# A hybrid delta-rule layer on one core: raw keys, a group's last tile recurred behind the next group's rows, output transpositions later, and the solve's 12 stores and 33 loads issued by GpSimd

## The chip, the core and the metric

The kernel runs on one core of one Trainium2 chip. The metric is the device time of one execution in microseconds (us). The core has a matrix engine (TensorE, PE in the profile), a vector engine (VectorE, DVE), a scalar engine (ScalarE, ACT), GpSimd (POOL) and a sync engine (SyncE, SP) that issues transfers. Each engine takes its own instructions in the order in which they were written for it, and waits for others by semaphores. ACT and POOL can issue transfers too.

## The reference

One layer of a streaming encoder, for 2048 prompt rows and 8 running streams of 16 rows. Only the gated delta rule and what feeds it is touched by the change:

```
P = rmsnorm(x) @ w_in                      # q, k, v, z, b, a, B, C, H
q, k, v = silu(causal_conv4(q, k, v))      # 4 heads x 128
q = l2norm(q) * 128 ** -0.5 ; k = l2norm(k) ; beta = sigmoid(b)
g = -exp(a_log) * softplus(a + dt_bias)
S_t = exp(g_t) (I - beta_t k_t k_t^T) S_{t-1} + beta_t k_t v_t^T ;  o_t = S_t^T q_t
o = rmsnorm_head(o) * silu(z)
y = B * causal_conv3(C * H)                # second half of the width
x = x + rmsnorm(concat(o, y) @ w_o)
x = x + rmsnorm((silu(rmsnorm(x) @ w_gate) * (rmsnorm(x) @ w_up)) @ w_down)
```

## The kernel before

**Tiles and groups.** The rows are cut into 17 tiles of 128: tiles 0 to 15 are the prompt, tile 16 the running streams. The first stage (projections, convolutions, delta rule, short convolution) goes over six groups of two or three tiles: [0, 1, 16], [2, 3, 4], [5, 6, 7], [8, 9, 10], [11, 12], [13, 14, 15]. I call them groups 0 to 5. Behind it come the output projection (`o_tile`, one tile at a time) and the feed-forward part with its two halves, over all tiles.

**A group.** `x_prep` loads the rows, normalises them and splits them in two parts (`hi`, `lo`) that together carry fp32 precision through the matrix engine. `gate_prep` makes the decays; its small products (weights `wba`) are the first that need the group's rows. Then 28 weight blocks are multiplied with the rows, 24 matrix instructions each, into the PSUM tiles `dbank` (line 139): four heads of k, of v and of q (`qkv_stage`), four blocks of z (`z_stage`), twelve of the short convolution (`sc_stage`). The weights are loaded three blocks ahead by SP (`weights`, `wsplit`); in groups 0, 1 and 4 some are split anew by ACT, DVE and POOL (lines 342 and 344).

**Keys.** For each head the convolved key (`kraw`) is transposed by PE into a PSUM tile `tbank` (line 427), ACT sums its squares (412), DVE, POOL and DVE make 1/sqrt times sqrt(beta) (131, 133, 430), DVE multiplies the tile with it (431), PE transposes the result back (435) and ACT copies that out (437).

**The solve.** `pair_stage` makes k k^T and k q^T for each tile (519, 520), multiplied with decays by DVE (523, 524). The 32 x 32 diagonal blocks go through DRAM (`sa`, then `As`) so that DVE can invert 48 of them at a time in 31 steps (539, 541). The inverses go back to DRAM in two layouts, `sT` and `sU` (542, 544), and are loaded per tile as `utd` (562, 556). `level_stage` joins the blocks on PE (568, 578, 579, 589, 594) to the whole inverse.

**The recurrence.** `chunk_stage` carries the state S from tile to tile: S against k (625), DVE makes `r` (627, 628), the inverse against r (632), ACT copies `yt` (634), POOL scales the keys (636), PE makes the new S (639, 642), and the output from S (646) and from `yt` (651). `out_stage` norms the output (605 to 612), PE transposes it (615), DVE multiplies with the gate (617), ACT stores it. `sample_stage` does the same for tile 16.

**The order.** The code is written in the order above, group by group. A scheduler then sets each engine's order by a timing model of its own, so that projections of one stretch stand between the short dependent products of another. The order is fixed when the program is built. Transfers of SP stand in one row: weights, rows, blocks of the solve.

Of the kernel before, what the change touches and what calls it, by code (L numbers as in the profile page):

```python
# [9 lines left out]
F32 = mybir.dt.float32  # L10
F32R = mybir.dt.float32r
BF16 = mybir.dt.bfloat16
AF = mybir.ActivationFunctionType
# [4 lines left out]
P = 128  # L18
# [18 lines left out]
NPD, NPT, NPG = 3, 2, 2  # L37
NR, NKV = 3, 3
XKB = 4
# [33 lines left out]
def kernel(  # L73
# [52 lines left out]
    neghalf = const.tile([P, 4 * MAXT], F32, name="neghalf")  # L126
    V.memset(neghalf, -0.5)

    def rstd(small, ss, n, scale, eps, tag):
# [14 lines left out]
    with ExitStack() as ph:  # L144
# [102 lines left out]
        def gate_prep(tiles, hi, lo, rb):  # L247
# [36 lines left out]
            v3 = lambda a: a.rearrange("p (t h) -> p t h", h=H)  # L284
            A.activation(v3(sb)[:, :n], sp3[:, :n, 0:4], AF.Exp, scale=-0.5)
            V.tensor_mul(v3(gg)[:, :n], sp3[:, :n, 4:8], nega.unsqueeze(1).broadcast_to([P, n, H]))
# [29 lines left out]
            for i, t in enumerate(tiles):  # L316
# [6 lines left out]
                dts.append(dt)  # L323
            return dict(sb=sb, eG=eG, tl=tl, eL=eL, eLs=eLs, dt=dts)

# [82 lines left out]

        def sumsq(ps, n, nm):
            ss = small.tile([P, n], F32, tag=nm, name=nm)  # L410
            for i in range(n):
                A.activation(junkq, ps[:, i * P:(i + 1) * P], AF.Square, accum_out=ss[:, i:i + 1])
            return ss

        def qkv_stage(tiles, hi, lo, rb, gt, pool):
            n = len(tiles)
            c = n * P
            kt = pool.tile([P, H, MAXT, P], F32, tag="kt", name="kt")
            vt = pool.tile([P, H, MAXT, P], F32, tag="vt", name="vt")
            kT, qT, ssq = [], [], []  # L420
            sb = gt["sb"].rearrange("p (t h) -> p t h", h=H)
            for h in range(H):
                raw = cp.tile([P, W1], F32, tag="kvT", name="kraw", bufs=NKV)
                conv_qkv(tiles, 4 + h, project(h, hi, lo, c), raw, rb)
                ps = tbank()
                for i in range(n):
                    T.transpose(ps[:, i * P:(i + 1) * P], raw[:, i * P:(i + 1) * P], ident)
# [3 lines left out]
                V.tensor_mul(kt[:, h, :n], ps[:, :c].rearrange("p (t d) -> p t d", d=P),  # L431
                             rk.unsqueeze(2).broadcast_to([P, n, P]))
                ps = tbank()
                for i in range(n):
                    T.transpose(ps[:, i * P:(i + 1) * P], kt[:, h, i, :], ident)
                o = pool.tile([P, W1], F32, tag="kT", name="kT", bufs=H)
                A.copy(o[:, :c], ps[:, :c])
                kT.append(o)
            for h in range(H):
                raw = cp.tile([P, W1], F32, tag="kvT", name="vraw", bufs=NKV)  # L440
                conv_qkv(tiles, 8 + h, project(4 + h, hi, lo, c), raw, rb)
                ps = tbank()
                for i in range(n):
                    T.transpose(ps[:, i * P:(i + 1) * P], raw[:, i * P:(i + 1) * P], ident)
                V.tensor_mul(vt[:, h, :n], ps[:, :c].rearrange("p (t d) -> p t d", d=P),
                             sb[:, :n, h].unsqueeze(2).broadcast_to([P, n, P]))
            for h in range(H):
# [5 lines left out]
                ssq.append(sumsq(ps, n, f"ssq{h}"))  # L453
                qT.append(o)
            gt.update(kt=kt, vt=vt, kT=kT, qT=qT, ssq=ssq)
# [53 lines left out]
        def pair_stage(tiles, gi, gt):  # L509
# [25 lines left out]
            for j in range(31):  # L535
# [5 lines left out]
                V.tensor_sub(Ts[:m, j + 1:32, 0:b], Ts[:m, j + 1:32, 0:b], p3)  # L541
            nc.sync.dma_start(out=sT[:n].rearrange("t h b j i -> (t h b) j i"), in_=Ts[:m])
            V.tensor_copy(As[:m].rearrange("p j i -> p i j"), Ts[:m])
            nc.sync.dma_start(out=sU[:n].rearrange("t h b j i -> (t h b) j i"), in_=As[:m])
            gt["sT"], gt["sU"] = sT, sU

        def level_stage(tiles, gt):
            gt["U"] = []
            for i, t in enumerate(tiles):
# [5 lines left out]
                ud, td = (utd[:, q].rearrange("p (h c) -> p h c", h=H) for q in range(2))  # L555
                nc.sync.dma_start(out=ud, in_=gt["sU"][i].rearrange("h b j i -> (b j) h i"))
# [5 lines left out]
                nc.sync.dma_start(out=td, in_=gt["sT"][i].rearrange("h b j i -> (b j) h i"))  # L562
                ps = bank()
# [38 lines left out]
        def out_stage(t, i, o, gt):  # L602
            sso = small.tile([P, H], F32, tag="sso", name="sso")
            for h in range(H):
                A.activation(junko, o[:, h, :], AF.Square, accum_out=sso[:, h:h + 1])
            e = small.tile([P, H], F32, tag="sqe", name="sqe")
            for h in range(H):
                V.tensor_scalar(out=e[:, h:h + 1], in0=gt["ssq"][h][:, i:i + 1], scalar1=EPS, scalar2=P * P * EPS,
                                op0=ALU.add, op1=ALU.mult)
            V.tensor_add(e, e, sso)  # L610
            f = rstd(small, e, H, 1.0 / P, 0.0, "of")
            V.tensor_mul(o, o, bc(f))
            ps = obank()
            for h in range(H):
                T.transpose(ps[:, h * P:(h + 1) * P], o[:, h, :], ident)
            ot = wk.tile([P, H, P], F32, tag="ot", name="ot")
            V.scalar_tensor_tensor(ot, h4(ps), g_hd, gt["sz"][:, :, i * P:(i + 1) * P], op0=ALU.mult, op1=ALU.mult)
            nc.scalar.dma_start(out=mixd[t][:, 0:4, :], in_=ot)

        def chunk_stage(t, i, gt, S):  # L620
# [24 lines left out]
            for h in range(H):  # L645
                T.matmul(ps[:, h * P:(h + 1) * P], gt["qT"][h][:, c0:c1], S[:, h, :], start=True, stop=True)
            o = wk.tile([P, H, P], F32, tag="o", name="o")
            V.tensor_mul(o, h4(ps), bc(eG))
            ps = obank()
            for h in range(H):  # L650
                T.matmul(ps[:, h * P:(h + 1) * P], gt["QK"][i][:, h, :], yt[:, h, :], start=True, stop=True)
            V.tensor_add(o, o, h4(ps))
            out_stage(t, i, o, gt)
            return Sn

        def sample_stage(t, i, gt):
# [10 lines left out]
            yt = wk.tile([P, H, P], F32, tag="yt", name="yts")  # L667
            o = wk.tile([P, H, P], F32, tag="o", name="os")
            for h in range(H):
# [19 lines left out]
                for q in range(2):  # L689
# [45 lines left out]
        for u in ubuf:  # L735
            G.memset(u, 0.0)

        for gi, tiles in enumerate(GROUPS):
            if gi:
                hi, lo, rb = *x_prep(tiles), None  # L740
            gt = gate_prep(tiles, hi, lo, rb)
            qkv_stage(tiles, hi, lo, rb, gt, gp if (len(GROUPS) - gi) % 2 else dp)
            pair_stage(tiles, gi, gt)
            level_stage(tiles, gt)
            z_stage(tiles, hi, lo, rb, gt)
            for i, t in enumerate(tiles):
                if t == SAMPLE:
                    sample_stage(t, i, gt)
                else:
                    S = chunk_stage(t, i, gt, S)  # L750
            sc_stage(tiles, hi, lo, rb)
            if SAMPLE in tiles:
                nc.scalar.dma_start(out=conv_s, in_=cch)
                nc.scalar.dma_start(out=sc_s, in_=sch)
        nc.scalar.dma_start(out=state_p, in_=S)
        nc.scalar.dma_start(out=conv_p, in_=hist)
# [571 lines left out]
```

## Time and profile before

| | us |
|---|---|
| median of 3 runs | 2602.99 (2598.48 to 2603.35) |
| the profiled execution | 2609.88 |
| its span, first to last instruction | 2608.1 |
| ACT busy in the span | 1033.2 (40%) |
| DVE busy in the span | 1748.9 (67%) |
| POOL busy in the span | 645.1 (25%) |

The span is what the trace covers; the 1.8 us around it belong to the start and end. The groups take the first 960 us, the output projection goes to about 1250, the feed-forward part to the end. A row of the view of waits reads: engine and line that waited, whom it waited for, us in total, how many times, the longest. In rows in order of time, the number in brackets is the engine's idle time just before.

### The profile page before, as it was taken

The numbers are of one execution on the slowest core, as the hardware profiler recorded it, in microseconds if no ns is written. First come the engines' busy times: TensorE is split into PE (matmuls) and PEld (weight loads), VectorE is DVE, ScalarE is ACT, GpSimd is POOL, SyncE is SP. The second block draws the span as 40 slices with busy tenths as digits, with TensorE's granted clock in tenths as the row PEclk, the third lists the DMA queues.
The fourth block names the chain that finished last, engine by engine and source line by source line (L and its number), as shares of the span: only waits on it lengthen the run. The fifth ranks groups of instructions, "written<-read, shape, count | busy, mean of one in ns | idle before, by whom it ended". The sixth has DMA issues, their size and how long they took to land.

```text
span 2608.1 us, 41962 instructions
## 1 busy us (share of the span) xinstructions
PE 2509.2 (96%) x15129; PEld 2337.4 (90%) x15129; DVE 1748.9 (67%) x3549; ACT 1033.2 (40%) x2496; POOL 645.1 (25%) x598
## 2 busy tenths in 40 slices
PE   8989999999989999999999999999999999999998
PEld 7989899999888988778999999999999988788786
DVE  7787766666587665777878864544655555677598
ACT  6545144261554423444434442222433335333343
POOL 3321101010120101214556620000000025555563
PEclk9999999999999999999999999999999999999999
DMA  7876575757567573768877788887988853443466
GB/s 266 297 267 238 193 268 198 246 193 237 193 205 247 184 233 129 234 216 287 291 253 271 264 281 259 280 246 244 295 272 296 275 176 106 125 125 122 128 216 185
DMA packets 320816, 589.42 MB, mean 226 GB/s; under 512 B 55533, under 2 KB 204721, under 8 KB 301793
## 3 DMA queue, kind: packets, MB, share of 16 engines
q1 hardware_dynamic: 182512, 509.28, 58.8%
q10 hardware_dynamic: 138096, 77.46, 9.8%
q8 instruction: 120, 1.97, 0.3%
q14 instruction: 88, 0.71, 0.1%
HBM read 424.60 MB, written 162.05 MB: 225 GB/s over the span
## 4 chain that ended last, share of the span: by engine, by line
PE 70%; DVE 11%; DMA 9%; ACT 4%; issue 3%; POOL 2%; ACTq 1%; SPq 0%; DVEq 0%; POOLq 0%
PE fbank L1010 32%; PE dbank L139 15%; PE fbank L1168 10%; PE tbank L794 3%; PE dbank L794 3%; DMA xk<-in_xT 1%; DVE xr L1187 1%; DMA dr<-in_w_dn 1%; DVE acc L370 1%; DMA xt<-in_x 1%; DVE acc L1127 1%; DMA w<-wsplit 1%; DVE Ts L541 1%; DMA partd<-pt 1%; DMA utd<-sT 1%
## 5 line engine op out<-in xcount | busy, mean ns | idle before, releaser
L1010 PE MATMUL fbank<-xh,fw 128*128 128x384 f32 (+1 forms) x3696 | 901.3, 327 | 9.4 <-ACT m L1044 4.4
L139 PE MATMUL dbank<-hi,w 128*128 128x384 f32 (+1 forms) x2688 | 685.3, 334 | 12.7 <-ACT w L342 6.0
L1010 PEld LDWEIGHTS fbank<-xh,fw 128*128 128x128 f32 x3696 | 653.2, 188 | 11.3 <-ACT m L1044 5.0
L1010 PE MATMUL fbank<-xl,fw 128*128 128x384 f32 (+1 forms) x1848 | 603.7, 327 | 0.0
L139 PEld LDWEIGHTS dbank<-hi,w 128*128 128x128 f32 x2688 | 480.8, 191 | 18.5 <-ACT w L342 6.0
L1168 PE MATMUL fbank<-dw,as 128*128 128x512 f32 x1980 | 458.8, 393 | 8.6 <-DVE acc L1127 2.5
L1168 PEld LDWEIGHTS fbank<-dw,as 128*128 128x128 f32 x1980 | 370.6, 188 | 96.5 <-DVE acc L1127 4.5
L139 PE MATMUL dbank<-lo,w 128*128 128x384 f32 (+1 forms) x1344 | 446.4, 332 | 1.1 <-DVE lo L228 1.1
L1010 PEld LDWEIGHTS fbank<-xl,fw 128*128 128x128 f32 x1848 | 348.1, 188 | 0.0
L139 PEld LDWEIGHTS dbank<-lo,w 128*128 128x128 f32 x1344 | 256.9, 191 | 3.7 <-DVE lo L228 1.7
L1152 POOL TENSOR_TENSOR as<-ar,as 128x256 fp32r<-128x256 f32 (+1 forms) x207 | 186.5, 911 | 277.7 <-ACT as L1149 276.9
L1127 DVE TENSOR_TENSOR acc<-acc,fbank 128x512 f32<-128x512 f32 x248 | 166.3, 682 | 93.4 <-PE fbank L1168 75.6
L867 POOL TENSOR_TENSOR dw<-dr,dw 128x512 fp32r<-128x512 f32 x52 | 77.3, 1498 | 484.6 <-ACT dw L865 484.4
L1149 ACT CAST as<-ar 128x256 fp32r<-128x256 f32 (+1 forms) x288 | 117.8, 427 | 181.3 <-PE fbank L1168 130.0
L985 ACT CAST fw<-rg 128x512 fp32r<-128x512 f32 x124 | 77.3, 623 | 188.9 <-PE fbank L1010 170.8
L370 DVE SCALAR_TENSOR_TENSOR acc<-R,cw,acc 128x384 f32<-128x384 f32 (+2 forms) x216 | 132.8, 620 | 12.8 <-ACT acc L401 8.8
L344 POOL TENSOR_TENSOR w<-wr,w 128x512 fp32r<-128x512 f32 x49 | 73.0, 1490 | 228.0 <-ACT w L342 170.5
L1057 DVE TENSOR_TENSOR c<-u,fbank 128x384 f32<-128x384 f32 (+1 forms) x66 | 34.9, 529 | 102.2 <-PE fbank L1010 102.0
L1053 DVE TENSOR_TENSOR m<-m,m 128x384 f32<-128x384 f32 (+1 forms) x44 | 23.1, 525 | 97.8 <-ACT m L1046 97.8
L539 DVE TENSOR_TENSOR pr<-As,Ts 48x31 f32<-48x31 f32 (+25 forms) x186 | 66.7, 359 | 29.8 <-DMA As<-sa 25.7
L342 ACT CAST w<-wr 128x512 fp32r<-128x512 f32 x98 | 56.4, 616 | 61.9 <-PE dbank L139 29.4
L1055 ACT ACTIVATE m<-fbank 128x384 f32<-128x384 f32 (+1 forms) x66 | 31.2, 473 | 121.5 <-PE fbank L1010 112.4
(358 smaller groups left out, 3708.3 us busy)
## 6 DMA issues: line engine op xcount, KB each, us to landing
w<-wsplit SPq DMA_DIRECT2D x119, 1024.0 KB, 5.3
fw<-fsplit SPq DMA_DIRECT2D x188, 512.0 KB, 4.8
fsplit<-fw SPq DMA_DIRECT2D x94, 512.0 KB, 4.0
partd<-pt ACTq DMA_DIRECT2D x88, 384.0 KB, 6.5
rg<-in_w_gu SPq DMA_DIRECT2D x62, 512.0 KB, 4.3
wsplit<-w SPq DMA_DIRECT2D x28, 1024.0 KB, 5.3
wr<-in_w_in SPq DMA_DIRECT2D x98, 256.0 KB, 3.9
ar<-partd SPq DMA_DIRECT2D x48, 384.0 KB, 3.3
```

The lines of the kernel that those rows point to most:

```text
L139: T.matmul(ps, l, r, start=(i == 0), stop=(i == n - 1))
L344: e.tensor_tensor(out=wl[:, c], in0=wr, in1=wh[:, c].bitcast(F32), op=ALU.subtract)
L370: V.scalar_tensor_tensor(acc, raw(d), w[:, d:d + 1], acc, op0=ALU.mult, op1=ALU.add)
L539: V.tensor_mul(p3, As[:m, j, j + 1:32].unsqueeze(2).broadcast_to([m, a, b]), Ts[:m, j, 0:b].unsqueeze(1).broadcast_to([m, a, b]))
L794: T.matmul(pss[n], m_[:, j, :], w_[k][:, n * 512:(n + 1) * 512], start=(k == 0 and ci == 0), stop=(k == KD - 1 and ci == 2))
L867: e.tensor_tensor(out=w[:, 1], in0=v, in1=w[:, 0].bitcast(F32), op=ALU.subtract)
L985: A.copy(w[:, 0], v)
L1010: T.matmul(ps, w_[:, c], b_[k][:, :hw], start=(first and k == 0 and ci == 0), stop=(k == KH - 1 and ci == 2), skip_group_check=not first)
L1127: V.tensor_add(dst, dst, ps)
L1149: ins = A.copy(a[:, 0, :n], v)
L1152: e.tensor_tensor(out=a[:, 1, :n], in0=v, in1=a[:, 0, :n].bitcast(F32), op=ALU.subtract)
L1168: T.matmul(ps, a[:, x_, q * P:(q + 1) * P], w[:, y_], start=(start and q == 0 and ci == 0), stop=(q == c - 1 and ci == 2), skip_group_chec ...
```

## The change

Four things, in the groups only.

**Raw keys.** The keys stay unnormed. The convolution writes them where `kT` was (no second transposition), ACT copies the first transposition into `kt`. The sums of squares of the four heads are collected; once per group DVE and POOL make c2 = beta / (|k|^2 + eps) and rt = sqrt(|k|^2 + eps). c2 is multiplied into `tl` (three small DVE instructions) and into the decay tiles `dt` (four ACT instructions for each tile, 68 in all), rt into v in place of sqrt(beta).

**Last tile later.** The last prompt tile of a group has its `chunk_stage` behind the next group's `x_prep` in the code, ahead of its `gate_prep`.

**Output transpositions later.** The end of `out_stage` (transposition, gate, store) is put in a list; the list is worked off behind the next tile's output, or behind the next group's key heads.

**Solve transfers.** Stores of `sT` and `sU` and loads of `utd` are issued by POOL instead of SP.

```
+        def sumsq(ps, n, ss):
             for i in range(n):
+                A.activation(junkq, ps[:, i * P:(i + 1) * P], AF.Square, accum_out=ss(i))
...
             for h in range(H):
-                raw = cp.tile([P, W1], F32, tag="kvT", name="kraw", bufs=NKV)
-                conv_qkv(tiles, 4 + h, project(h, hi, lo, c), raw, rb)
+                o = pool.tile([P, W1], F32, tag="kT", name="kT", bufs=H)
+                conv_qkv(tiles, 4 + h, project(h, hi, lo, c), o, rb)
                 ps = tbank()
                 for i in range(n):
-                    T.transpose(ps[:, i * P:(i + 1) * P], raw[:, i * P:(i + 1) * P], ident)
-                ss = sumsq(ps, n, "ssk")
-                rk = rstd(small, ss, n, 1.0, EPS, "rk")
-                V.tensor_mul(rk, rk, sb[:, :n, h])
-                V.tensor_mul(kt[:, h, :n], ps[:, :c].rearrange("p (t d) -> p t d", d=P),
-                             rk.unsqueeze(2).broadcast_to([P, n, P]))
-                ps = tbank()
-                for i in range(n):
-                    T.transpose(ps[:, i * P:(i + 1) * P], kt[:, h, i, :], ident)
-                o = pool.tile([P, W1], F32, tag="kT", name="kT", bufs=H)
-                A.copy(o[:, :c], ps[:, :c])
+                    T.transpose(ps[:, i * P:(i + 1) * P], o[:, i * P:(i + 1) * P], ident)
+                sumsq(ps, n, lambda i: ssk[:, 4 * i + h:4 * i + h + 1])
+                A.copy(kt[:, h, :n], ps[:, :c].rearrange("p (t d) -> p t d", d=P))
                 kT.append(o)
+            V.tensor_scalar_add(ssk[:, :m], ssk[:, :m], EPS)
+            G.tensor_tensor(out=rt[:, :m], in0=ssk[:, :m], in1=half[:, :m], op=ALU.pow)
+            V.reciprocal(c2[:, :m], ssk[:, :m])
+            V.tensor_mul(c2[:, :m], c2[:, :m], gt["beta"][:, :m])
+            V.tensor_mul(gt["tl"][:, :m], gt["tl"][:, :m], c2[:, :m])
+            flush()
             for h in range(H):
...
                 V.tensor_mul(vt[:, h, :n], ps[:, :c].rearrange("p (t d) -> p t d", d=P),
-                             sb[:, :n, h].unsqueeze(2).broadcast_to([P, n, P]))
+                             rt3[:, :n, h].unsqueeze(2).broadcast_to([P, n, P]))
+                if h < n:
+                    for g in range(H):
+                        A.mul(gt["dt"][h][:, g, :], gt["dt"][h][:, g, :], c2[:, 4 * h + g:4 * h + g + 1])
...
-            nc.sync.dma_start(out=sT[:n].rearrange("t h b j i -> (t h b) j i"), in_=Ts[:m])
+            nc.gpsimd.dma_start(out=sT[:n].rearrange("t h b j i -> (t h b) j i"), in_=Ts[:m])
...
-                nc.sync.dma_start(out=td, in_=gt["sT"][i].rearrange("h b j i -> (b j) h i"))
+                nc.gpsimd.dma_start(out=td, in_=gt["sT"][i].rearrange("h b j i -> (b j) h i"))
...
+            def turn():
+                ps = obank()
+                ...
+            turns.append(turn)
+        def flush():
+            while turns:
+                turns.pop(0)()
...
             V.tensor_add(o, o, h4(ps))
+            flush()
             out_stage(t, i, o, gt)
...
+        held = None
         for gi, tiles in enumerate(GROUPS):
             if gi:
                 hi, lo, rb = *x_prep(tiles), None
+                S = chunk_stage(*held, S)
...
             for i, t in enumerate(tiles):
                 if t == SAMPLE:
                     sample_stage(t, i, gt)
-                else:
+                elif i != last:
                     S = chunk_stage(t, i, gt, S)
+            held = tiles[last], last, gt
             sc_stage(tiles, hi, lo, rb)
+        S = chunk_stage(*held, S)
+        flush()
```

`sU` and its loads change as `sT` does, and the output tile `o` has two buffers where it had one. The buffer count of `kvT` goes from 3 to 2.

**Place 1, the solve's transfers in group 1.** On SP before, `sT`, `sU` and the `utd` loads stand between weights (`w`, `wr`) and the last rows (`xk`) of the next group; `wsplit` is the stored split of a weight block.

```order
L205 DMA xk<-in_xT 128x384
L542 DMA sT_3213<-Ts 48x1024
L544 DMA sU_3214<-As 48x1024
L341 DMA wr<-in_w_in 128x512
L349 DMA wsplit_104<-w_4145 128x2048
L562 DMA utd<-sT_3213 128x4x32
L556 DMA utd<-sU_3214 128x4x32 x2
L562 DMA utd<-sT_3213 128x4x32
L334 DMA w_4184<-wsplit_77 128x2048
L341 DMA wr<-in_w_in 128x512
L334 DMA w_4214<-wsplit_78 128x2048
L205 DMA xk<-in_xT 128x384
```

On POOL after, the same transfers stand ahead of a weight split (346), the memsets of `level_stage` (592), the root `rt` of the next group's keys (435) and the scaled keys `kl` of the recurrence (652).

```order
L549 DMA sT_3159<-Ts 48x1024
L551 DMA sU_3160<-As 48x1024
L569 DMA utd<-sT_3159 128x4x32 x2
L563 DMA utd<-sU_3160 128x4x32 x2
L346 TENSOR_TENSOR w_4019<-wr,w_4019 128x512
L592 MEMSET AU 32x4x32
L563 DMA utd<-sU_3160 128x4x32
L569 DMA utd<-sT_3159 128x4x32
L592 MEMSET AU 32x4x32 x2
L435 TENSOR_TENSOR rt<-ssk,half 128x12
L652 TENSOR_TENSOR kl<-kt,tl 128x512
```

SP has lost the rows that wait for the solve, and POOL has gained them; the weight split behind them belongs to the next group.

**Place 2, the end of group 1 on PE (tile 4).** Before, the output product (651), the next group's pair products (519, 520) and the output's transposition (615) stand close together; 179 spreads the row norms of group 3.

```order
L139 MATMUL dbank<-hi,w_5000 128x384
L179 MATMUL tbank<-rg,cst 128x384
L651 MATMUL obank<-yt,dt 128x128 x4
L520 MATMUL gbank<-qT,kT 128x128 x4
L519 MATMUL gbank<-kT 128x128 x4
L520 MATMUL gbank<-qT,kT 128x128 x4
L615 MATMUL obank<-cst,o 128x128 x4
L646 MATMUL obank<-S,qT 128x128 x4
```

After, the output product is line 667, the pair products are 526 and 527, the transposition is 624. Between the last row of the first piece and the first of the second stand 15 further projection matmuls.

```order
L655 MATMUL gbank<-yt,kl 128x128 x4
L667 MATMUL obank<-yt,dt 128x128 x4
L526 MATMUL gbank<-kT 128x128 x4
```

```order
L527 MATMUL gbank<-qT,kT 128x128 x3
L624 MATMUL obank<-cst,o 128x128 x4
L527 MATMUL gbank<-qT,kT 128x128
L526 MATMUL gbank<-kT 128x128 x4
L141 MATMUL dbank<-hi,w_4918 128x384
L141 MATMUL dbank<-lo,w_4918 128x384
L141 MATMUL dbank<-hi,w_4918 128x384 x2
L141 MATMUL dbank<-lo,w_4918 128x384
L141 MATMUL dbank<-hi,w_4918 128x384
L527 MATMUL gbank<-qT,kT 128x128 x4
L624 MATMUL obank<-cst,o 128x128 x4
```

The first 624 is tile 3's, the second tile 4's: between a tile's output product and its transposition there are now 21 projection matmuls and five sets of four short products. The tile's recurrence itself stood beside the next group's pair products before, and stands there now.

**Place 3, the ends of groups 3 and 0 on PE after.** First tile 10 (group 3), whose transposition is the last 624 here.

```order
L655 MATMUL gbank<-yt,kl 128x128 x4
L526 MATMUL gbank<-kT 128x128 x4
L667 MATMUL obank<-yt,dt 128x128 x4
L527 MATMUL gbank<-qT,kT 128x128 x4
L526 MATMUL gbank<-kT 128x128 x4
L624 MATMUL obank<-cst,o 128x128 x4
L527 MATMUL gbank<-qT,kT 128x128 x4
L181 MATMUL tbank<-rg,cst 128x384
L624 MATMUL obank<-cst,o 128x128 x4
L662 MATMUL obank<-S,qT 128x128 x4
```

Then tile 1 (group 0), whose chain 641, 648, 655, 667 stands without a projection in it.

```order
L641 MATMUL gbank<-S,kT 128x128 x4
L181 MATMUL tbank<-rg,cst 128x384
L662 MATMUL obank<-S,qT 128x128 x4
L648 MATMUL gbank<-r,ubuf_213 128x128 x4
L655 MATMUL gbank<-yt,kl 128x128 x4
L667 MATMUL obank<-yt,dt 128x128 x4
L526 MATMUL gbank<-kT 128x128 x4
L527 MATMUL gbank<-qT,kT 128x128 x4
```

In tile 10 four sets of short products stand between 667 and its 624. In tile 1 one set and a spread stand between 641 and 648, nothing between 648 and 655; before, 14 to 36 projection matmuls stood in each such gap of the groups 0 to 4.

More of the change, by code (lines that the diff above doesn't have):

```diff
@@ L37 @@
 NPD, NPT, NPG = 3, 2, 2
-NR, NKV = 3, 3
+NR, NKV = 3, 2
 XKB = 4
@@ L127 @@
     V.memset(neghalf, -0.5)
+    half = const.tile([P, 4 * MAXT], F32, name="half")
+    V.memset(half, 0.5)
     def rstd(small, ss, n, scale, eps, tag):
@@ L284, in gate_prep @@
             v3 = lambda a: a.rearrange("p (t h) -> p t h", h=H)
-            A.activation(v3(sb)[:, :n], sp3[:, :n, 0:4], AF.Exp, scale=-0.5)
+            A.activation(v3(sb)[:, :n], sp3[:, :n, 0:4], AF.Exp, scale=-1.0)
             V.tensor_mul(v3(gg)[:, :n], sp3[:, :n, 4:8], nega.unsqueeze(1).broadcast_to([P, n, H]))
@@ L323, in gate_prep @@
                 dts.append(dt)
-            return dict(sb=sb, eG=eG, tl=tl, eL=eL, eLs=eLs, dt=dts)
+            return dict(beta=sb, eG=eG, tl=tl, eL=eL, eLs=eLs, dt=dts)
         wloads = []
@@ L407, in conv_qkv @@
                 A.activation(dst[:, pc:c].rearrange("p (s l) -> p s l", s=NS), segments(acc, pc, 0, 3 + LS)[:, :, 3:], AF.Silu)
-        def sumsq(ps, n, nm):
-            ss = small.tile([P, n], F32, tag=nm, name=nm)
+        def sumsq(ps, n, ss):
             for i in range(n):
-                A.activation(junkq, ps[:, i * P:(i + 1) * P], AF.Square, accum_out=ss[:, i:i + 1])
-            return ss
+                A.activation(junkq, ps[:, i * P:(i + 1) * P], AF.Square, accum_out=ss(i))
         def qkv_stage(tiles, hi, lo, rb, gt, pool):
@@ L452, in qkv_stage @@
                     T.transpose(ps[:, i * P:(i + 1) * P], o[:, i * P:(i + 1) * P], ident)
-                ssq.append(sumsq(ps, n, f"ssq{h}"))
+                ss = small.tile([P, MAXT], F32, tag=f"ssq{h}", name=f"ssq{h}")
+                sumsq(ps, n, lambda i: ss[:, i:i + 1])
+                ssq.append(ss)
                 qT.append(o)
@@ L541, in pair_stage @@
                 V.tensor_sub(Ts[:m, j + 1:32, 0:b], Ts[:m, j + 1:32, 0:b], p3)
-            nc.sync.dma_start(out=sT[:n].rearrange("t h b j i -> (t h b) j i"), in_=Ts[:m])
+            nc.gpsimd.dma_start(out=sT[:n].rearrange("t h b j i -> (t h b) j i"), in_=Ts[:m])
             V.tensor_copy(As[:m].rearrange("p j i -> p i j"), Ts[:m])
-            nc.sync.dma_start(out=sU[:n].rearrange("t h b j i -> (t h b) j i"), in_=As[:m])
+            nc.gpsimd.dma_start(out=sU[:n].rearrange("t h b j i -> (t h b) j i"), in_=As[:m])
             gt["sT"], gt["sU"] = sT, sU
@@ L555, in level_stage @@
                 ud, td = (utd[:, q].rearrange("p (h c) -> p h c", h=H) for q in range(2))
-                nc.sync.dma_start(out=ud, in_=gt["sU"][i].rearrange("h b j i -> (b j) h i"))
+                nc.gpsimd.dma_start(out=ud, in_=gt["sU"][i].rearrange("h b j i -> (b j) h i"))
                 for b in range(4):
@@ L612, in out_stage @@
             V.tensor_mul(o, o, bc(f))
[L613 to L618, printed above, removed]
+            def turn():
+                ps = obank()
+                for h in range(H):
+                    T.transpose(ps[:, h * P:(h + 1) * P], o[:, h, :], ident)
+                ot = wk.tile([P, H, P], F32, tag="ot", name="ot")
+                V.scalar_tensor_tensor(ot, h4(ps), g_hd, gt["sz"][:, :, i * P:(i + 1) * P], op0=ALU.mult, op1=ALU.mult)
+                nc.scalar.dma_start(out=mixd[t][:, 0:4, :], in_=ot)
+            turns.append(turn)
+        turns = []
+        def flush():
+            while turns:
+                turns.pop(0)()
         def chunk_stage(t, i, gt, S):
@@ L646, in chunk_stage @@
                 T.matmul(ps[:, h * P:(h + 1) * P], gt["qT"][h][:, c0:c1], S[:, h, :], start=True, stop=True)
-            o = wk.tile([P, H, P], F32, tag="o", name="o")
+            o = wk.tile([P, H, P], F32, tag="o", name="o", bufs=2)
             V.tensor_mul(o, h4(ps), bc(eG))
@@ L667, in sample_stage @@
             yt = wk.tile([P, H, P], F32, tag="yt", name="yts")
-            o = wk.tile([P, H, P], F32, tag="o", name="os")
+            o = wk.tile([P, H, P], F32, tag="o", name="os", bufs=2)
             for h in range(H):
@@ L745 @@
             z_stage(tiles, hi, lo, rb, gt)
+            last = max(i for i, t in enumerate(tiles) if t != SAMPLE)
             for i, t in enumerate(tiles):
@@ L754 @@
                 nc.scalar.dma_start(out=sc_s, in_=sch)
+        S = chunk_stage(*held, S)
+        flush()
         nc.scalar.dma_start(out=state_p, in_=S)
```

6 lines of the change are left out of this document (5 added, 1 removed).

## The prediction

> **What bounds the kernel now.** I read the page's busy times first, then stretches of the span, then PE's waits.
>
> ```profile
> span 2608.1 us, 41962 instructions
> PE 2509.2 (96%) x15129; PEld 2337.4 (90%) x15129; DVE 1748.9 (67%) x3549; ACT 1033.2 (40%) x2496; POOL 645.1 (25%) x598
> ```
>
> PE does nothing in only 99 us of 2608. In the table of stretches the columns are: stretch, length, then busy time of PE, PEld, DVE, ACT, POOL, the granted clock, the transfers' share, GB/s.
>
> ```profile
> 0.00:960.00 960.00, 905.97 (x6417) 862.51 (x6417) 660.62 (x1791) 421.37 (x1131) 143.29 (x143) 0.98 0.69 231
> 1250.00:2608.00 1358.00, 1331.92 (x7278) 1242.32 (x7276) 890.62 (x1399) 494.80 (x1084) 435.71 (x387) 0.99 0.70 224
> ```
>
> The six groups hold 54 us of the idle time, and only they are changed. What PE does after 1250 us stays as it is, so whatever the groups gain or lose moves the end by as much. PE's own waits, as far as they lie in the groups and bear on the change:
>
> ```profile
> PE tbank L139 <- ACT hi L209: 12.0, 4, 8.0
> PE dbank L139 <- DMA w<-wsplit: 5.9, 5, 2.6
> PE tbank L435 <- DVE kt L431: 4.3, 6, 2.5
> PE obank L615 <- DVE R L391: 3.5, 1, 3.5
> PE obank L615 <- DVE o L612: 3.2, 1, 3.2
> PE tbank L427 <- DVE tl L307: 1.7, 1, 1.7
> PE obank L646 <- DVE ot L617: 0.8, 1, 0.8
> ```
>
> A wait costs more than its length, which short stretches right behind four of them show:
>
> ```profile
> 167.30:172.90 5.60, 5.42 (x19) 4.57 (x20) 4.07 (x8) 1.77 (x4) 2.80 (x4) 0.56 0.80 210
> 455.30:462.80 7.50, 6.66 (x27) 6.42 (x26) 4.91 (x16) 1.25 (x3) 0.00 (x0) 0.54 0.19 61
> 684.40:687.70 3.30, 3.30 (x47) 2.85 (x47) 2.91 (x9) 2.15 (x6) 0.00 (x0) 0.52 0.14 40
> 722.40:725.90 3.50, 3.47 (x20) 3.50 (x21) 3.50 (x13) 2.02 (x4) 0.00 (x0) 0.61 0.76 183
> 64.50:67.90 3.40, 3.36 (x22) 3.40 (x23) 3.33 (x8) 2.32 (x7) 1.01 (x1) 1.00 0.91 310
> ```
>
> Behind the waits of 8.0, 3.2, 2.4 and 3.5 us (in this order; the first and third are two of the four of line 139 for `hi`) the granted clock is about half for 3 to 7 us. PE's busy time there times what is missing of the clock is the tail: 5.42 x 0.44 = 2.4, 6.66 x 0.46 = 3.1, 3.30 x 0.48 = 1.6, 3.47 x 0.39 = 1.4 us. Behind the 2.5 us wait of line 435, the last row, there was none.
>
> [...]
>
> **The change part by part.**
>
> *Second key transpositions.* 68 go (four heads of 17 tiles).
>
> ```profile
> 210.85 0.49 PE L435 MATMUL tbank<-cst,kt 128*128 128x128 f32 x3
> 211.18 0.49 PE L427 MATMUL tbank<-cst,kraw 128*128 128x128 f32 x3
> ```
>
> Three start 0.33 us ahead of what follows, so 0.11 each: 68 x 0.11 = **7.5 us**, all on PE. With them goes their wait, **4.3 us** (no tail): what it waited for, the norm between two transpositions, exists no more. DVE loses 24 products, ACT exchanges one copy for another:
>
> ```profile
> L431 DVE TENSOR_TENSOR kt<-tbank,rkr x24: 411/554/559, 53.3 to 874.5; 128x384 f32<-128x384 f32 x20, 128x256 f32<-128x256 f32 x4
> L412 ACT ACTIVATE junkq<-tbank x136: 255/277/320, 41.7 to 897.3; 128x128 bf16<-128x128 f32 x136
> ```
>
> That is 13 us less for DVE. ACT gains 68 scalings of `dt`; the nearest row of that size is 412, 0.28 us, so 19 us more in the 539 us that it has free of 960. They stand between v and q heads, with the projections of those as cover, and I cost them at nothing; without that cover it is 0.28 us each, at most 19.
>
> *Output transpositions.* At tile 4 PE came to them too early:
>
> ```profile
> 447.85 1.05 PE L651 MATMUL obank<-yt,dt 128*128 128x128 f32 x8
> 448.94 0.69 DVE L652 TENSOR_TENSOR o<-o,obank 128x512 f32<-128x512 f32 x1 [0.51 <-PE obank L651]
> 454.95 0.66 PE L615 MATMUL obank<-cst,o 128*128 128x128 f32 x4 [3.21 <-DVE o L612]
> ```
>
> From 448.94 to 454.95 the norm's chain takes 6.0 us. In the new order 21 projection matmuls and five sets stand there. By rows of this trace a 128x384 projection goes at 0.18 us (43.4 us for 240 in the chain) and a set of four at about 0.9 (448.74 to 449.63), together 21 x 0.18 + 5 x 0.9 = 8.3 us: enough.
>
> ```profile
> 458.52 43.40 PE dbank L139 x240
> 448.74 1.06 PE L520 MATMUL gbank<-qT,kT 128*128 128x128 f32 x8
> 449.63 1.06 PE L519 MATMUL gbank<-kT 128*128 128x128 f32 x8
> ```
>
> So 3.2 + 0.8 (the next product waited for the same bank) + tail 3.1, and at 722 us 3.5 + 1.4: **12.0 us** go. But at tile 10 the new order has only four sets, 3.6 us, for 6.0: a new wait of 2.4 and a tail of 1.6, **-4.0**. And tile 1's chain has no projection in it:
>
> ```profile
> L628 DVE TENSOR_TENSOR r<-vt,r x16: 672/692/695, 210.1 to 1007.0; 128x512 f32<-128x512 f32 x16
> L634 ACT COPY yt<-gbank x16: 566/586/597, 214.9 to 1013.7; 128x512 f32<-128x512 f32 x16
> ```
>
> Two products of 0.69 on DVE against one set, then a copy of 0.59 with nothing: 0.5 + 0.6, with hand-overs about **-2.0** in all. Nothing else of PE waits ahead of its turn there, since it is PE itself that stands.
>
> *The last tile behind the next rows.* Place 2 shows that the scheduler had already put tile 4's recurrence among the next group's pair products. I give this part nothing of its own.
>
> *Transfers on POOL.* SP waited for the solve with weights and rows queued behind:
>
> ```profile
> SPq L556 <- PE gbank L579: 22.7, 5, 6.6
> SPq L542 <- DVE Ts L541: 18.0, 6, 5.6
> SPq L562 <- DMA sT<-Ts: 8.0, 4, 2.8
> ```
>
> These 49 us of standing leave SP. Behind them stood the `xk` rows that the 12.0 us of group starts waited for, and weight loads (5.9). Not all was SP: at 167 us DVE was late too. I take half: of 12.0 + 2.4 + 1.6 (tails) + 1.7 (line 427, DVE late at a start) = 17.7, **8.9**; of 5.9, **3.0**. The ends are nothing and all, 0 to 23.6.
>
> In return POOL waits. Behind its store and loads stand a weight split, memsets, `rt` and `kl`, for which DVE's v products and the recurrence wait. And the first product of the level stage comes right behind its load:
>
> ```profile
> 503.18 0.92 ACT L573 COPY AU<-utd 32x128 f32<-32x128 f32 x3 [9.02 <-DMA utd<-sT]
> 503.54 0.44 PE L568 MATMUL gbank<-utd,AU 32*32 32x32 f32 x16
> L562 SPq DMA_DIRECT2D utd<-sT x16: 370/498/1118, 169.5 to 953.5; - x16
> utd<-sT SPq DMA_DIRECT2D x16, 64.0 KB, 4.6
> sT<-Ts SPq DMA_DIRECT2D x5, 192.0 KB, 3.9
> mixd<-ot ACTq DMA_DIRECT2D x17, 256.0 KB, 2.5
> ```
>
> The slack there is 0.4 us. No row shows a transfer issued by POOL. From below: on a queue without weight loads, ACT's, 256 KB land in 2.5 us where SP's took 3.9 and 4.6, so the chain can be 3.5 us shorter; PE's place is fixed, so that wins nothing. From above: an issue that costs as much as POOL's long operations, and stands while DVE runs, as these show:
>
> ```profile
> 720.47 1.26 POOL L344 TENSOR_TENSOR w<-wr,w 128x512 fp32r<-128x512 f32 x1
> L612 DVE TENSOR_TENSOR o<-o,ofr x16: 684/692/1749, 229.7 to 1032.1; 128x512 f32<-128x512 f32 x16
> L543 DVE COPY As<-Ts x6: 1021/1116/1121, 165.0 to 936.9; 48x1024 f32<-48x1024 f32 x5, 32x1024 f32<-32x1024 f32 x1
> ```
>
> The 1749 ns of line 612 fell on that POOL operation: the two keep each other out. Three issues of 1.3 instead of 0.5, and 1.1 for the copy at 543 right behind the solve, make 3.5 us, with a tail of 1.5 up to 5 a group. I take **-1.5 a group, -9.0**, near the lower end, since the shorter landing stands against it; ends 0 and -30.
>
> [...]
>
> **The sum.** 7.5 + 4.3 + 12.0 + 8.9 + 3.0 = 35.7 won; 4.0 + 2.0 + 9.0 = 15.0 lost; 20.7 less. The profiled execution took 2609.9 us (span 2608.1 and 1.8 around it), 6.9 above the median of the runs, 2603.0. So 2589 under the profiler and **2582 us** as a median.
>
> **The rivals.**
>
> *Moved waits (0.22).* The static order is new everywhere, and DVE (69% of the groups) and ACT set when PSUM tiles come free; other waits take the place of those at starts and transpositions. For it: the waits are many and short, and places 2 and 3 already show two new ones. Against it: DVE gets 13 us back. Then 7.5 + 4.3 remain, less 9.0: 2600.
>
> *POOL is late (0.14), the slower side.* One mechanism: store, landing and first load are issued in a row on POOL, and each late group start stops PE at 568. It decides when lateness with its tail of 1.5 eats (35.7 - 6.0) / 6 = 5.0 us, so from 3.5 us a group, the upper end above. At 5 us a group: 29.7 - 6 x 6.5 = -9, **2612**. Against it: landing in 2.5 us.
>
> *All goes (0.16).* Group starts and weight waits go wholly and POOL's landing pays for its issue: 7.5 + 4.3 + 12.0 + 17.7 + 5.9 - 6.0 = 41.4, 2562.
>
> **How the numbers follow.** The forecast has 0.48, 2582 with its own 2572 to 2594. The range goes from 2562 to 2610 and leaves out part of the slower rival and what is beyond 41 us. 0.2% (5 us) is about what a measurement can tell from no change. Faster: 0.48 + 0.16 + half of the moved waits, 0.75; within: the other half, 0.11; slower 0.14.
>
> **What would show it.** Right: no PE row at a second key transposition, PE's busy time some 7 us or more less, no wait at tile 4's transposition, one of 2 to 3 us at tile 10's, SP without rows that wait for `Ts`. Wrong: PE waiting at 575 (568 before) in each group, POOL's issues above 1.3 us, or `tbank` waits of the v products for `rt`. If the first stretch of 960 us shrinks by less than 10, the moved waits are the case; if it grows, POOL is.

## The result, and the profile after

The changed kernel took 2647.03 us (median of 4 runs, 2645.08 to 2648.51), the kernel before 2603.17 beside it: a ratio of **1.0153** (95% interval 1.0129 to 1.0178), 1.5% or about 40 us slower. The forecast was 2582, the range ended at 2610.

The page's span and busy times of the changed kernel:

```profile
span 2646.7 us, 41835 instructions
PE 2522.9 (95%) x15061; PEld 2349.9 (89%) x15061; DVE 1740.7 (66%) x3502; ACT 1060.0 (40%) x2568; POOL 672.8 (25%) x625
```

Its first 1010 us in the view of stretches (columns as in the prediction):

```profile
0.00:1010.00 1010.00, 926.88 (x6463) 880.20 (x6464) 653.19 (x1754) 451.94 (x1211) 171.84 (x171) 0.95 0.64 222
```

PE has 68 instructions less and is still busy for 13.7 us more, and the granted clock is 0.95 where it was 0.98. I cut the first 1010 us of both traces into stretches of 2.5 us and added up what PE stood and what the clock took (busy time times what the clock lacks of 1). Before: 56.7 us stood, 14.4 lost to the clock. After: 83.1 and 36.9. That is 26.4 + 22.5 more; less 7.5 for the transpositions it makes 41.4, and the span grew by 38.6. **Nearly half of the loss is the lower clock**, not the waits themselves. That the clock falls behind the waits is seen at single places (a clock of 0.57 from 525 to 541 us, below); for the whole sum it is argued.

PE's waits in the first 1000 us after, the larger ones (the row left out is the start of the kernel):

```profile
PE tbank L141 <- ACT hi L211: 13.4, 3, 6.6
PE dbank L141 <- DMA w<-wsplit: 9.0, 5, 2.7
PE tbank L263 <- ACT bsb L260: 7.6, 2, 7.4
...
PE tbank L446 <- ACT kt L430: 4.8, 3, 2.8
PE gbank L526 <- DVE AU L530: 4.7, 2, 4.4
PE gbank L585 <- DMA utd<-sU: 4.4, 1, 4.4
PE gbank L585 <- ACT xs L577: 3.8, 1, 3.8
PE gbank L575 <- DMA utd<-sT: 3.4, 2, 2.0
PE dbank L141 <- POOL w L346: 2.9, 2, 2.7
PE obank L624 <- DVE o L619: 2.6, 2, 2.1
```

The first product behind a load (575) waits 3.4 us in all, little. The larger waits are for ACT (`hi`, `bsb`, `xs`) and for `sU`. Not all of them are new: of the 13.4 us for `hi`, 6.6 are the start of group 1 at 168.33, before any load has landed, and before the change that start waited 8.0. The rows of POOL at group 2's solve show what stands behind the others:

```profile
511.19 0.81 POOL L569 DMA_DIRECT2D utd<-sT  x1 [1.60 <-DMA sT<-Ts]
517.30 0.78 POOL L569 DMA_DIRECT2D utd<-sT  x1 [5.29 <-DMA mixd<-yo]
524.07 0.75 POOL L563 DMA_DIRECT2D utd<-sU  x1 [6.00 <-issue]
526.72 0.76 POOL L563 DMA_DIRECT2D utd<-sU  x1 [1.90 <-issue]
533.60 0.75 POOL L563 DMA_DIRECT2D utd<-sU  x1 [5.91 <-issue]
536.67 0.76 POOL L569 DMA_DIRECT2D utd<-sT  x1 [2.32 <-issue]
```

"issue" in brackets is time for which the profile shows no cause. Each load costs 0.75 us of POOL, but the next starts 2.7 to 6.9 us later. In the view of POOL's waits over all groups, these are 24 of the 33 loads and 80.2 us:

```profile
POOL utd L563 <- issue: 40.9, 15, 6.4
POOL utd L569 <- issue: 39.3, 9, 6.9
```

ACT's rows at group 2 show where it stops: it copies each load as it lands (566, 580).

```profile
523.84 0.61 ACT L580 COPY AU<-utd 32x128 f32<-32x128 f32 x2 [6.22 <-DMA utd<-sT]
524.48 1.12 ACT L211 ACTIVATE hi<-xk,vec 128x384 fp32r<-128x384 f32 x2
...
526.44 1.22 ACT L566 COPY ubuf<-utd 32x128 f32<-32x128 f32 x4 [0.28 <-DMA utd<-sU]
527.69 0.61 ACT L211 ACTIVATE hi<-xk,vec 128x384 fp32r<-128x384 f32 x1
533.32 0.30 ACT L566 COPY ubuf<-utd 32x128 f32<-32x128 f32 x1 [5.01 <-DMA utd<-sU]
```

A load has landed by 523.84, where ACT starts to copy it, and POOL issues the next at 524.07; one lands by 526.44, the next goes at 526.72; one lands by 533.32, the next goes at 533.60. **In these rows POOL starts a load 0.23 to 0.28 us after ACT has begun to copy the one before.** And the next group's `hi` stand on ACT behind the copies. PE's rows that wait for a load or for what stands behind one, without the shorter waits:

```profile
363.79 1.01 PE L141 MATMUL dbank<-hi,w 128*128 128x384 f32 x2 [2.70 <-POOL w L346]
526.55 0.22 PE L585 MATMUL gbank<-xs,utd 32*32 32x32 f32 x2 [4.40 <-DMA utd<-sU]
535.22 0.50 PE L141 MATMUL tbank<-hi,wba 128*16 128x384 f32 x1 [5.71 <-ACT hi L211]
695.47 0.31 PE L585 MATMUL gbank<-xs,utd 32*32 32x32 f32 x2 [3.85 <-ACT xs L577]
859.24 0.50 PE L263 MATMUL tbank<-cst,bsb 16*128 16x16 f32 x3 [7.44 <-ACT bsb L260]
```

The weight split that the first row waits for stands on POOL right behind a load that was issued at 361.70. The stretch around the second and third row:

```profile
525.00:541.00 16.00, 8.74 (x61) 6.39 (x62) 5.92 (x13) 6.39 (x19) 2.48 (x4) 0.57 0.36 108
```

In these 16 us PE worked for 8.7 at a clock of 0.57. The wait of 7.4 us for `bsb`, the last row, is the same thing in group 4: ACT copies the `sU` load that lands at 854.66 and the one at 857.28, and only then comes `bsb` at 858.52.

From the solve's last instruction on DVE to the last product of the group's inverses on PE, groups 1 to 5, it took 56.7, 56.1, 46.6, 38.2, 30.4 us before and 64.8, 70.5, 63.7, 51.9, 38.7 after. The last of these products stood at 967.1 and stands at 1008.4: 41.3 us later, which covers the whole loss.

The landings, from the view of transfers (issue to landing, median us):

```profile
utd<-sU POOLq DMA_DIRECT2D x17, 64.0 KB, 2.4
utd<-sT POOLq DMA_DIRECT2D x16, 64.0 KB, 3.1
sT<-Ts POOLq DMA_DIRECT2D x5, 192.0 KB, 6.4
```

Once issued, a load lands sooner than SP's (4.0 and 4.6), the store later (3.9).

### The profile page after: what moved, and what is told of

Same layout as the page of the kernel before. It is cut to its first block, busy times and chain, and to the rows that moved or that the text cites. A ratio compares the mean times of both kernels' runs of the same rounds, so it can differ in the third digit from the quotient of the medians.

```text
span 2646.7 us, 41835 instructions
## 1 busy us (share of the span) xinstructions
PE 2522.9 (95%) x15061; PEld 2349.9 (89%) x15061; DVE 1740.7 (66%) x3502; ACT 1060.0 (40%) x2568; POOL 672.8 (25%) x625
## 4 chain that ended last, share of the span: by engine, by line
PE 53%; DVE 10%; DMA 7%; issue 6%; ACT 2%; POOL 2%; ACTq 1%; SPq 0%; DVEq 0%; POOLq 0%
PE fbank L1034 31%; PE fbank L1192 10%; PE dbank L141 4%; PE tbank L818 2%; PE dbank L818 2%; DVE xr L1211 1%; DVE acc L1151 1%; POOL dw L891 1%; DMA partd<-pt 1%; DMA xt<-in_x 1%; DMA xk<-in_xT 1%; DMA hTd<-ht 0%; DVE acc L372 0%; DVE pr L546 0%; DMA dr<-in_w_dn 0%
## 5 line engine op out<-in xcount | busy, mean ns | idle before, releaser
L141 PE MATMUL dbank<-hi,w 128*128 128x384 f32 (+1 forms) x2688 | 698.1, 339 | 19.3 <-DMA w<-wsplit 9.0
L141 PEld LDWEIGHTS dbank<-hi,w 128*128 128x128 f32 x2688 | 490.6, 195 | 28.1 <-issue 8.8
L141 PE MATMUL dbank<-lo,w 128*128 128x384 f32 (+1 forms) x1344 | 453.7, 338 | 0.7 <-DVE lo L230 0.7
L344 ACT CAST w<-wr 128x512 fp32r<-128x512 f32 x98 | 56.7, 615 | 69.9 <-PE dbank L141 36.8
```

The lines of the kernel that those rows point to most:

```text
L141: T.matmul(ps, l, r, start=(i == 0), stop=(i == n - 1))
```

## The experiments

The theory from these rows, P: POOL's loads cost it, one behind the landing of the other. Against it stood O, the new static order that the held tile makes, and K, the raw keys' 68 scalings and four copies on ACT.

All ratios are to runs of the kernel before on the same chip at the same time (medians 2608 to 2610 there), so ratios are compared, not microseconds. "Stood" and "clock" are the two sums of above.

| run | raw keys | held tile | later transp. | transfers | ratio (95% interval) | stood | clock |
|---|---|---|---|---|---|---|---|
| before | | | | SP | 1 | 56.7 | 14.4 |
| after | x | x | x | POOL | 1.0153 (1.0129 to 1.0178) | 83.1 | 36.9 |
| e1_sp | x | x | x | SP | 0.9989 (0.9975 to 1.0003) | 56.6 | 20.3 |
| e2_pool | | | | POOL | 1.0200 (1.0182 to 1.0219) | 87.8 | 27.9 |
| e3_raw_sp | x | | | SP | 1.0055 (1.0038 to 1.0073) | 67.7 | 25.9 |
| e4_nohold | x | | x | POOL | 1.0181 (1.0164 to 1.0198) | 86.0 | 32.8 |
| e5_raw_turns | x | | x | SP | 1.0003 (0.9989 to 1.0017) | 62.4 | 19.2 |
| e6_raw_hold | x | x | | SP | 1.0052 (1.0035 to 1.0070) | 68.5 | 23.2 |
| e11_norm_sp | | x | x | SP | 1.0015 (0.9999 to 1.0030) | 57.9 | 13.0 |

### Which of the four parts

**e1_sp**, the transfers back on SP (`sU`, `ud` and `td` as `sT`):

```
-            nc.gpsimd.dma_start(out=sT[:n]...
+            nc.sync.dma_start(out=sT[:n]...
```

> The changed kernel with the four solve transfers issued by SP again; raw keys, held tile and later transpositions stay. Theory P (each load on POOL starts only when the one before has landed, 2.4 to 6.9 us apart, and ACT, DVE and the hi tiles queue behind): the loss of 44 us goes, 2590 to 2605 us, no wait of PE for utd, PE idle in the first 1010 us back from 83 to under 60. Rival O (the new order of the held tile makes the waits): 2630 or more. Rival K (68 more scalings and four copies on ACT make hi late): 2625 or more, with the waits for hi of 5 us and above still there.

Measured 0.9989: the loss is gone, and the rivals' 2625 and 2630 did not come. PE stands as long as before. Apart from the start of the kernel one long wait is left, at the start of group 1. The view of PE's waits puts it down to a load, but the product at 173.00 needs `hi`, which ACT starts at 172.34, behind three stores of `yo` that stand there for 4.4 us from 167.85:

```profile
PE tbank L141 <- DMA utd<-sT: 9.7, 1, 9.7
```

ACT's rows there:

```profile
167.85 4.43 ACTq L514 DMA_DIRECT2D mixd<-yo  x3
172.34 1.63 ACT L211 ACTIVATE hi<-xk,vec 128x384 fp32r<-128x384 f32 x3 [5.99 <-DMA mixd<-yo]
```

**e2_pool**, the kernel before with the same four lines the other way.

> The kernel before with nothing but the four solve transfers issued by POOL. Theory P: 2630 to 2650, PE waits for utd, POOL stands some 80 us in its 33 loads. Rivals O and K: within 8 us of 2603.

Measured 1.0200, 52 us: more than expected, and more than the whole change. POOL's waits, as far as they have no cause in the profile:

```profile
POOL utd L556 <- issue: 48.6, 15, 7.2
POOL utd L562 <- issue: 37.8, 9, 7.1
```

86 us in 24 loads, against 80.2 in the changed kernel. Theory P holds, though its number was too low.

One thing these two runs do not part: with another issuer the scheduler also makes another order. Some 820 of PE's 15061 products stand in another place in e1_sp than in the changed kernel, and as many between e2_pool and the kernel before. For the loads and against the order speaks that all four kernels with whole loads on POOL are slow, each in its own order (1.0153 to 1.0200, e4 and e9 below), while no kernel with the loads on SP is above 1.0055. How much of the 43 or 52 us is the order's remains open.

**e3_raw_sp**, only the raw keys, and **e4_nohold**, the change without the held tile:

```
-                elif i != last:
+                else:
                     S = chunk_stage(t, i, gt, S)
...
-        S = chunk_stage(*held, S)
```

> The kernel before with nothing but the raw keys (transfers on SP, no held tile, transpositions at once). Theory P: 7.5 us of transpositions and up to 4.3 of their wait go, 2591 to 2603. Rival K: 2615 or more, ACT behind. Rival O says nothing against 2591 to 2603.

> The changed kernel without the held tile: the last tile's recurrence stands in its own group again; transfers stay on POOL. Theory P: within 10 us of 2647. Rival O: 2600 to 2615. Rival K: within 10 us of 2647 too.

e4 at 1.0181 is as theory P has it; the held tile does not cause the loss. But e3 is a miss of theory P's number: 1.0055, 14 us slower, though PE has 68 instructions less. Rival K's sign was right there, though K missed e1.

### Which transfers, and why

**e8_stpool** and **e9_ldpool** split the four lines: stores on POOL and loads on SP, and the reverse. PE's order in e8 is that of e1_sp but for one small product, so between these two little but the issuer of the stores differs.

> The changed kernel with the 33 loads of utd on SP again, the 12 stores on POOL; PE's order is that of e1_sp. Theory L (the loads cost it, one behind the landing of the other): within 8 us of e1_sp, 2598 to 2614. Rival S (the store costs it: sT landed in 6.4 us from POOL against 3.9 from SP, six times 2.5, with clock tails): 2618 to 2630.

> The changed kernel with the 12 stores on SP again, the 33 loads of utd on POOL. Theory L: 2635 to 2655, POOL standing some 80 us in its loads. Rival S: 2618 to 2630.

e8: 1.0002 (0.9985 to 1.0018), e9: 1.0166 (1.0139 to 1.0192). The stores cost nothing measurable, though `sT` lands in 6.5 us there; the loads cost everything.

**e10_half** cuts each load in two of half the partitions:

```
-                nc.gpsimd.dma_start(out=ud, in_=...)
+                for z in range(2):
+                    nc.gpsimd.dma_start(out=ud[64 * z:64 * z + 64], in_=...)
```

> The changed kernel with each of the 33 loads of POOL cut in two of half the partitions (256 pieces of 128 bytes each, 32 KB). If POOL takes a load only when the one before has landed, whatever its size: 66 waits of 2.4 us and more, 2670 to 2700. If it holds so many pieces (some 512) at a time: the halves are taken two by two, 2635 to 2660.

Measured 1.0068 (1.0044 to 1.0093), faster than either theory had it: twice as many transfers of POOL took 22 us less than the change. POOL's rows at two of the solves (a load of `sT` is line 572 here, "x3" is three in a row):

```profile
167.75 1.90 POOL L572 DMA_DIRECT2D utd<-sT  x3 [5.36 <-DMA sT<-Ts]
173.08 0.63 POOL L572 DMA_DIRECT2D utd<-sT  x1 [3.42 <-issue]
...
827.15 1.89 POOL L572 DMA_DIRECT2D utd<-sT  x3 [1.68 <-DMA sT<-Ts]
833.64 0.61 POOL L572 DMA_DIRECT2D utd<-sT  x1 [4.61 <-issue]
```

Three halves go at once, in each of the six groups, and the fourth stands 2.1 to 4.6 us. So it is neither one transfer at a time nor two halves, as the two theories had it: three loads of 32 KB go in a row in 1.9 us, a fourth does not, and of whole loads (64 KB) a second does not. Bytes alone do not part them either: in e13 below, three stores of 64 KB go in a row in 1.6 us. By the kernel's access patterns a whole load has 512 pieces of 128 bytes, a half 256, such a store 128 of 512 bytes. On SP's queue the trace shows the pieces of a load (528 packets, 512 and 16), on POOL's it shows 32 packets for a load and 32 for a half. What decides how many go in a row, these runs do not show.

### What the other parts do

> The kernel before with the held tile and the later transpositions alone (keys normed as before, transfers on SP, two kvT buffers). e3_raw_sp against e1_sp says that these two are worth 17 us: if they are worth that without the raw keys too, 2590 (2582 to 2598). If the raw keys and the held tile only pay together: 2600 to 2615.

> The kernel before with raw keys and the later output transpositions, transfers on SP, no held tile. Raw keys alone were +14, raw keys with both others -3. If the later transpositions bring the 17 us back (they take the waits for the output's norm away): 2600 to 2610. If the held tile does: 2618 to 2630.

> The kernel before with raw keys and the held tile, transfers on SP, transpositions at once. If the later transpositions bring the 17 us back: 2618 to 2630. If the held tile does: 2600 to 2610.

e11 took 1.0015: without raw keys, the held tile and the later transpositions win nothing. e5 1.0003 and e6 1.0052: with raw keys it is the later transpositions that bring the 14 us back, and the held tile does nothing. The gain from e3 to e1 does not belong to the two edits by themselves, but to the raw keys and the later transpositions together.

Three edits look for what eats the raw keys' gain. **e12_kt_dve**, in e1_sp:

```
-                A.copy(kt[:, h, :n], ps[:, :c]...)
+                V.tensor_copy(kt[:, h, :n], ps[:, :c]...)
```

> e1_sp with the 24 copies of the transposed keys made by DVE instead of ACT. If the raw keys' gain was eaten by ACT, which frees tbank late (in e1_sp PE waits 11 us in all for kt, vraw and qT of ACT): 2592 to 2600. If ACT's lateness is only where the order ends and not its cause: within 5 us of e1_sp.

**e14_raw_nkv3**, in e3_raw_sp: `NKV` 3 again and one tile `o`. **e15_dt_pool**, in e3_raw_sp:

```
-                    for g in range(H):
-                        A.mul(gt["dt"][h][:, g, :], gt["dt"][h][:, g, :], c2[...])
+                    G.tensor_tensor(out=gt["dt"][h], in0=gt["dt"][h], in1=bc(c2[...]), op=ALU.mult)
```

> e3_raw_sp with three kvT buffers and one output tile o, as in the kernel before. If the lost buffer of kvT makes v's convolutions wait: 2600 to 2612. If not: within 5 us of e3_raw_sp, which was 14 above the kernel before.

> e3_raw_sp with the decay tiles scaled by POOL, one product of 128 x 512 for each tile, in place of 68 scalings by ACT. If these scalings hold ACT up between the heads (19 us of ACT's time by the row of 0.28): 2603 to 2615, fewer waits of PE for vraw and kt. If not: within 5 us of e3_raw_sp.

e12: 0.9992 (0.9977 to 1.0007), as e1_sp. e14: 1.0048 (1.0018 to 1.0077), e15: 1.0043 (1.0028 to 1.0058), both as e3_raw_sp within their intervals. None of the three suspects is it.

### A version below both

**e13_yo_pool**, e1_sp with the 68 stores of `yo` on POOL, and **e16_before_yo**, the same line in the kernel before:

```
-                    nc.scalar.dma_start(out=mixd[t][:, 4 + b, :], in_=yo[...])
+                    nc.gpsimd.dma_start(out=mixd[t][:, 4 + b, :], in_=yo[...])
```

> e1_sp with the 68 stores of yo issued by POOL instead of ACT (128 pieces of 512 bytes each). In e1_sp PE waits 9.7 us for the first hi of group 1, behind three such stores that stand on ACT for 4.4 us. If those stores hold ACT up: 2590 to 2600, this wait below 6. If POOL's own issue hurts as with the loads: 2610 or more.

> The kernel before with the 68 stores of yo issued by POOL. If what e13_yo_pool won over e1_sp (8 to 9 us) is ACT freed of standing in its issues, it is won here as well: 2596 to 2605. If it was won only with the new order: within 4 us of the kernel before.

e13: **0.9954** (0.9933 to 0.9976), median 2597.68 beside 2610.31: faster than both kernels. Its rows of POOL at the start of group 1:

```profile
159.59 1.63 POOL L514 DMA_DIRECT2D mixd<-yo  x3 [0.94 <-DVE pr L546]
171.20 1.60 POOL L514 DMA_DIRECT2D mixd<-yo  x3
```

And PE's waits for `hi` in all groups of e13:

```profile
PE tbank L141 <- ACT hi L211: 3.4, 3, 2.2
```

The wait of 9.7 us is gone, the longest for `hi` is 2.2, as expected of ACT freed; and three stores of 128 pieces each go in 1.6 us without standing. But the profiled executions do not show the gain in the groups. Other waits came there (7.9 us for `wsplit` where e1_sp has 3.4), PE stood 59.8 us in the first 1010 us where it stood 56.6, and the last product of the inverses starts at 965.2 where it started at 961.7. The output projection, which the edit does not touch, then ends earlier, its last product at 1187.3 against 1191.2; PE waits 4.5 us between 965 and 1200 where e1_sp waits 10.7. Why is open. e16: 0.9999 (0.9986 to 1.0012): in the kernel before the edit wins nothing, and its wait for `hi` stays 7.8. So the gain does not come with this edit alone, as the second theory of e16 had it; what in the new order it hangs on is not shown.

## Why the prediction was wrong

**The step that failed first** is the price of POOL's transfers: "Three issues of 1.3 instead of 0.5, and 1.1 for the copy at 543 right behind the solve, make 3.5 us", taken as -1.5 a group and -9.0 in all, with -30 as the end. Against it stood 8.9 + 3.0 won on SP, so the whole part was to win 2.9 us. From 0.9989 to 1.0153 it cost 0.0164 x 2603 = 43 us, 7.1 a group. The durations were right (0.53 to 1.31 for the stores, 0.75 to 0.82 for a load), and so was the landing: 2.4 us for a load of `sU` where ACT's rows had given 2.5. What no row of before held is how long POOL stands in front of a load with the one before still under way: 80.2 us in 24 loads of the changed kernel. I bounded an unknown issue by its own length, and not by the wait in front of it.

**The place was wrong too.** The rival "POOL is late" had the sign, and at its price (6.5 a group with the tail) nearly the size. But it put the stop at line 575, which waits 3.4 us in all. ACT copies every load in its turn, and the next group's `hi` and `bsb` stand behind the copies. By the rows, the waits that hang on the loads are 3.4 at 575, 4.4 for `sU`, 3.8 for `xs`, 7.4 for `bsb`, 6.8 of the 13.4 for `hi` (at 179.54 and 535.22) and 2.7 for the weight split on POOL: 28.5 us, where PE stood 26.4 more. The prediction counted what stands behind the transfers on POOL, which made 2.7, not what stands behind their readers.

**DVE does not explain the loads.** The upper end of the price had an issue on POOL stand while DVE runs, from one row of before: line 612 on DVE took 1749 ns, where its median is 692, beside the POOL operation at 720.47. That row shows DVE standing and not POOL, whose operation took 1.26 us, the shortest of the 49 of line 344. In the changed kernel DVE had nothing to do between these two rows, while POOL stood from 518.08 to 524.07.

```profile
517.32 0.41 DVE L504 TENSOR_SCALAR acc<-u,scw 128x384 f32<-128x384 f32 x1
525.12 0.62 DVE L212 SCALAR_TENSOR_TENSOR lo<-xk,vec,hi 128x384 fp32r<-128x384 f32 x1 [7.38 <-ACT hi L211]
```

The five stores of `sT` that ran beside the copy at 550 landed 4.9 to 7.7 us after their issue, the sixth, which did not, in 4.3. But e8, with the stores alone on POOL, took 1.0002.

**The gains were wrong as well**, and the loss on POOL hid that. Without the transfers, and so without the 8.9 + 3.0 that were to be won on SP, the sum would have been 7.5 + 4.3 + 12.0 - 4.0 - 2.0 = 17.8 less; e1_sp gave 0.11%, 3 us. Term by term, by PE's waits:

- *Second transpositions, 7.5.* Right: from the kernel before to the changed one, busy time less the clock's loss fell by 8.8 us.
- *Their wait, 4.3.* It went, and others came in its place: all waits of PE at transpositions of k, v and q are 10.5 us before, 10.2 in e3_raw_sp and 12.5 in e1_sp, now for ACT's `kt`, `vraw` and `qT`.
- *Output transpositions, 12.0 less 6.0.* The mechanism was right: 6.7 us of waits at line 615 became 0.5 in e1_sp. In the changed kernel tile 10 waited 2.1 us at 789.24, where 2.4 was forecast, and tile 1's chain 0.5 and 0.8. But the recurrence's own products waited 6.7 us in e1_sp where they had waited 1.5.
- *Group starts, half of 17.7, and weights, half of 5.9.* These were to go with what left SP's queue. It left, and they stayed: with all the solve's transfers on POOL the start of group 1 waits 8.0 us in e2_pool, as before, and 6.6 in the changed kernel, and the weights wait 7.4 and 9.0 where they had waited 5.9. So SP's queue, to which I gave these waits, did not hold them. In e1_sp that start waits 9.7, behind ACT's stores of `yo`; in e13, without these stores on ACT, this wait is gone.

"Moved waits" was the right rival for all that is not POOL: its 7.5 + 4.3 was still 9 too much. PE stood 56.7 us before and 56.6 in e1_sp, and the clock took 6 more.

**Open:** why raw keys alone cost 14 us. The two sums say how (11.0 more stood, 11.5 more lost to the clock, less 7.5), spread over level stage, recurrence, weights and sample stage. That it is the new static order is argued, by e5 and e6, where another edit of the order takes it away. It is not shown.

## What to carry over

Before a transfer is given to another issuer, ask how long that issuer stands in front of it (here up to 6.9 us in front of a whole load, and not at all in front of the second and third of the half loads), and which engine reads the landing in its program order: what stood behind that reader paid here, with most of the 28.5 us of waits. A wait that is taken from an engine in a fixed order is a gain only when the next one due there has been named; here the three edits without the transfers were to take 4.3 + 12.0 - 6.0 = 10.3 us of waits and tails away, and the engine stood as long as before. And wherever waits cost clock, count both: nearly half of this loss was clock (22.5 us beside the 26.4 that PE stood longer).

## What the hardware did that I had not expected

**How many transfers POOL issued in a row differed with their form.** Whole loads of 64 KB went one by one, and a second one stood for up to 6.9 us. Half loads of 32 KB went three in a row in 1.9 us, and a fourth stood for 2.1 to 4.6 us. Stores of 64 KB went three in a row in 1.6 us. Neither the number of transfers nor their bytes tell the three apart; what does, these runs do not show.

**The clock was 0.51 behind two waits under 2 us, and 1.00 behind a longer one.** In the changed kernel two waits of 1.73 (to 50.87) and 1.54 us (to 57.17) stand six us apart:

```profile
52.50:62.50 10.00, 8.15 (x31) 7.46 (x31) 5.47 (x18) 9.62 (x29) 3.75 (x3) 0.51 0.44 157
809.10:815.00 5.90, 3.29 (x27) 3.32 (x28) 3.85 (x10) 1.70 (x4) 0.00 (x0) 1.00 1.00 336
```

The clock was 0.51 for 10 us, while behind one of 2.69 us, which ends at 811.71 in the second row, it stayed at 1.00. The length of a wait alone does not say whether a tail follows; what does, these runs do not show.
